# Seven-product block pairs in the w_out product of a two-layer decoder trunk

## The chip, the cores and the metric

The kernel runs on one core of a Trainium2 chip. The metric is the device time of one execution in microseconds; the median of three runs of the kernel before is 1481.37 us.

## The reference

One sequence of 512 tokens, model width 1024, passes two layers, and a last RMSNorm. All inputs are float32. Cut to what matters here:

```
h = rmsnorm(x, g_mix);  z = h @ w_in      # q, k, v | ret q, k, v, g | gate_a | gate_b
A = sliding-window attention(q, k, v)     # width 512
r = retention(ret q, k, v), normed per head, * silu(g)   # width 1024
mixed = sigmoid(gate_a) * (A @ w_a) + sigmoid(gate_b) * (r @ w_b)
x = x + mixed @ w_out                     # 1024 x 1024: the product that is changed
x = x + relu(rmsnorm(x, g_mlp) @ w_up)**2 @ w_down       # 1024 -> 4096 -> 1024
```

## The kernel before

**Layout.** Activations lie transposed: 128 rows of the width on the partitions, 512 tokens along a row. A width of 1024 is eight chunks of 128 rows (`KD = 8`), and a product makes one output chunk of 128 x 512 in one PSUM bank by eight steps over the chunks of its input.

**Three products for one.** Every operand is split into a high and a low part of fewer bits (`split`, and `split_until` for the weights: ScalarE writes the high part, VectorE the rest). `products` multiplies high by high, high by low and low by high, so a step is three matmuls with 512 columns, and an output chunk is 24 of them. The large products take most of the time.

**Weights.** `unit_order` lists all weight units (128 x 1024 numbers, 512 KB) in the order of their use. `unit` hands out the next one and has the following ones loaded (`load_until`, on SyncE's queue) and split (`split_until`) up to three ahead. Raw units, high parts and low parts have three buffers each, so the split of a unit waits until TensorE has done with the one three places earlier. `chunk` makes one output chunk from a unit, `group` four chunks together from four units, `two_chunks` two chunks from two units.

**Block pairs in the up product.** A pair of output chunks over the input's two halves and the tokens' two halves is a 2 x 2 block product. `narrow_pair` forms it from seven half-size products instead of eight, in the Winograd form of Strassen's scheme: sums and differences of weight blocks (`add_part`, VectorE), of input blocks (`sum_input`, kept in slots as `by_form`), and seven products of four steps with 256 columns, added up in three banks a, b and e. After a's first product ScalarE copies a into b, so that b goes on from it. The kernel uses this for one pair of w_up in each layer; `wide_pair` is a variant with a different split of operands, for the other pairs. The four weight parts of a pair come from two raw units.

**The stage around the change, in each layer.** `values` and the retention end; then four chunks of gate_b (`gate`, kept in `gates`), the first half of w_b as a group, four more gate chunks, and the second half of w_b as four chunks. `put_mixed` makes m, the mixed output, from each w_b chunk (in a temporary of its own) and splits it into slots (`ms`). x has served as storage for the gated attention (`mixed`) and is read back from memory for the residual. Then w_out: a group of four chunks and four single chunks. `put_x` adds a chunk to x, scales and splits it as the next input (`scaled_input`: ScalarE and VectorE), and adds up its squares (`squared_input`). Sums of x for the up product follow, then a group of four w_up chunks during which the inverse RMS is formed (`Rms.finish`, a reciprocal on VectorE), then the pairs of w_up among chunks of w_down.

**Order.** The order of instructions on each engine is set when the program is built: a scheduler of the framework places what the program issues, by its own estimates. On the chip each engine goes through its list in that order. Large buffers (`big`, 128 x 2 x 512) come from a pool of six, slots from nine tiles of four (`Slots`).

Of the kernel before, what the change touches and what calls it, by code (L numbers as in the profile page):

```python
# [12 lines left out]
F32R = mybir.dt.float32r  # L13
# [39 lines left out]
BETWEEN = (0, 2, 4, 5)  # L53


def unit_order():

    order = [("w_in", i) for i in range(4 + 2 + 8 + 2 + 4 + 2)]
    order += [("w_in", i) for i in range(22, 26)]
    order += [("w_a", i) for i in range(4)]  # L60
    order += [("w_in", i) for i in range(26, 42)]
    order += [("w_b", i) for i in range(4)]
    order += [("w_in", i) for i in range(42, 46)]
    order += [("w_b", i) for i in range(4, 8)]
    order += [("w_out", i) for i in range(8)]
    for what, q, i in mlp_sequence():
        if what == "first":
            order += [("w_up", u) for u in range(4)]
        elif what == "pair":
            order += [("pair", 8 * q + 2 * i, part) for part in range(4)]  # L70
        elif what == "down":
            order += [("w_down", 8 * q + 2 * i + u) for u in range(2)]
        else:
            order += [("w_down", 8 * q + u) for u in range(8)]
    return order
# [48 lines left out]
def decoder(ctx, tc, xT, x_first, w_in, w_a, w_b, w_out, w_up, w_down, tables, decay, band, triangles, g_last, out):  # L124
# [17 lines left out]
    def big(name, dtype=F32):  # L142
        return tmp.tile([P, 2, T], dtype, tag="big", name=name, bufs=6)
# [16 lines left out]
    slots = Slots([const.tile([P, 4, T], F32R, name=f"r{i}") for i in range(9)])  # L160
# [43 lines left out]
    def load_part(i):  # L204
        layer, _, j, part = order[i]
        if part == 0:
            raws[i] = raw_tile()
            nc.sync.dma_start(raws[i][:, LEFT], w_up[layer, j][:, LEFT])
            raws[i + 3] = raw_tile()
            nc.sync.dma_start(raws[i + 3], w_up[layer, j + 1])  # L210
        elif part == 1:
            raws[i] = big("raw2").rearrange("p a t -> p (a t)")
            nc.sync.dma_start(raws[i][:, RIGHT], w_up[layer, j][:, RIGHT])
# [15 lines left out]
    def split_until(n):  # L229
        while state["split"] < min(n, len(order)):  # L230
# [6 lines left out]
            if homes and i >= len(order) - len(homes):  # L237
                home = homes[len(order) - 1 - i]
                hi, lo = (home[:, 2 * a : 2 * a + 2, :].rearrange("p a t -> p (a t)") for a in range(2))
            else:  # L240


                first = (ASIDE, ASIDE) if paired else (0, 0)
                if paired and wide(order[i][2]):
# [266 lines left out]
    def layer_body(layer):  # L511
# [3 lines left out]
        def rstd():  # L515
            return rms_mix.value

# [474 lines left out]
        gates = []  # L992

        def gate_tile(c):
            if c % 2 == 0:
                two = big("gb")
                gates.extend(two[:, j, :] for j in range(2))
# [30 lines left out]

        source = xT if layer == 0 else spill
        for c in range(KD):  # L1030
            nc.sync.dma_start(x[:, c, :], source[:, c, :])

        def put_x(c):
            def put(ps):
                nc.vector.tensor_tensor(x[:, c, :], x[:, c, :], ps, ALU.add)
                scaled_input(c, g_mlp)
                squared_input(c, g_mlp)
# [14 lines left out]
        H = T // 2  # L1052
        sums = [slots.four() for _ in range(4)]
        by_form = [
            t[0].rearrange("p a (b t) -> p (a b) t", t=H).rearrange("p (j k s) t -> p j k s t", k=2, s=2) for t in sums
        ]

        def parts_of_forms(ks, j):
            t = by_form[2 * (j // 2) + ks // 2]
            return [t[:, :, :, s, :] for s in range(2)]  # L1060

        def sum_input(ks):

            b = [big("xg") for _ in range(2)]
            for i in range(2):
                for part, g in ((0, ks + i), (1, ks + i + 4)):
                    col = g_mlp * KD + g
                    nc.scalar.activation(b[part][:, i, :], x[:, g, :], AF.Copy, scale=gain[:, col : col + 1])
            (b11, b12), (b21, b22) = ((t[:, :, :H], t[:, :, H:]) for t in b)
            f = [big("sums").rearrange("p a (b t) -> p (a b) t", t=H) for _ in range(2)]  # L1070
            t1, t2, t3, t4 = f[0][:, 0:2, :], f[0][:, 2:4, :], f[1][:, 0:2, :], f[1][:, 2:4, :]
            nc.vector.tensor_tensor(t1, b12, b11, ALU.subtract)
            nc.vector.tensor_tensor(t2, b22, t1, ALU.subtract)
            split(*parts_of_forms(ks, 0), f[0].rearrange("p (j k) t -> p j k t", k=2))
            nc.vector.tensor_tensor(t3, b22, b12, ALU.subtract)
            nc.vector.tensor_tensor(t4, b21, t2, ALU.subtract)
            split(*parts_of_forms(ks, 2), f[1].rearrange("p (j k) t -> p j k t", k=2))

        def form(j):
            return [by_form[2 * (j // 2) + k // 2][:, j % 2, k % 2, :, :] for k in range(4)]  # L1080

        def block(half, tokens):
            at = slice(tokens * H, tokens * H + H)
            return [xhl[:, :, k, at] for k in range(4 * half, 4 * half + 4)]
# [19 lines left out]

        def narrow_pair(pool, step):
            def multiply(ps, weights, left, moving, start=True):
                hi, lo = weights
                cols = [slice((0 if left else 4 * P) + k * P, (0 if left else 4 * P) + (k + 1) * P) for k in range(4)]
                pairs = [((hi[:, c], lo[:, c]), (m[:, 0, :], m[:, 1, :])) for c, m in zip(cols, moving)]
                products(ps, pairs, start, True, not start)  # L1110

            b, a, e = (bank(pool, "mm")[:, :H] for _ in range(3))
            eu, z = temp("eu"), big("z")
            part = unit("pair", layer)
            multiply(a, part, True, block(0, 0))
            ins = nc.scalar.activation(b, a, AF.Copy).ins  # L1120
            step(ins)
            multiply(e, part, False, form(0))
            ins = nc.scalar.activation(eu[:, :H], e, AF.Copy).ins
            step(ins)
            part = unit("pair", layer)
            multiply(b, part, True, form(1), False)
            ins = nc.scalar.activation(eu[:, H:], b, AF.Copy).ins
            step(ins)
            multiply(a, part, False, block(1, 0), False)
            ins = nc.vector.scalar_tensor_tensor(z[:, 0, :H], a, 0.0, rms_mlp.value[:, :H], ALU.max, ALU.mult).ins  # L1130
            step(ins)
            part = unit("pair", layer)
            multiply(b, part, True, form(2), False)
            ins = nc.vector.tensor_tensor(z[:, 1, H:], b, eu[:, :H], ALU.add).ins  # L1134
            step(ins)
            multiply(e, part, False, block(1, 1), False)
            ins = nc.vector.tensor_tensor(z[:, 0, H:], e, eu[:, H:], ALU.add).ins
            step(ins)
            part = unit("pair", layer)
            multiply(b, part, True, form(3), False)  # L1140
            later = rms_mlp.value[:, H:].unsqueeze(1).broadcast_to([P, 2, H])
            nc.vector.scalar_tensor_tensor(z[:, :, H:], z[:, :, H:], 0.0, later, ALU.max, ALU.mult)
            nc.vector.scalar_tensor_tensor(z[:, 1, :H], b, 0.0, rms_mlp.value[:, :H], ALU.max, ALU.mult)
            return z
# [66 lines left out]
        def pair(q, i, late):  # L1211
# [11 lines left out]
            z = wide_pair(c == FIRST_WIDE + 2, i == 0 and q > 1, pool, step) if wide(c) else narrow_pair(pool, step)  # L1223
# [19 lines left out]
        def first_hooks():  # L1243
            def at1():
                rms_mlp.finish()
                sum_input(2)

            return {0: lambda: (rms_mlp.prepare(), sum_input(0)), 1: at1}

        for what, q, i in mlp_sequence():  # L1250
            if what == "first":
                late = group("w_up", layer, xs, [put_up] * 4, first_hooks())
            elif what == "pair":
                pair(q, i, late)
                if (q, i) == (3, 3):
                    for t in sums:
# [52 lines left out]
def _w_in_units(w):  # L1309
# [24 lines left out]
    units += _units_chunks(w, O_GB + r(D))  # L1334
    return units

# [55 lines left out]
def _laid_out(x, g_mix, w_in, sinks, w_a, w_b, w_out, g_mlp, w_up, w_down, g_final):  # L1392
# [13 lines left out]
        "w_b": _stack(w_b, _half_grouped),  # L1406
        "w_out": _stack(w_out, _half_grouped),
# [26 lines left out]
```

## Time and profile before

| what | value |
|---|---|
| runs | 1482.1, 1481.3, 1481.37 us; median 1481.37 us |
| profiled execution, first to last instruction | 1480.1 us |
| instructions of the profiled execution | 18928 |
| TensorE busy | 1473.5 us, 100% |
| TensorE loading weights | 1240.8 us, 84% |
| VectorE busy | 1097.6 us, 74% |
| ScalarE busy | 765.1 us, 52% |
| mean granted TensorE clock | 0.999 |
| HBM | 102 GB/s over the span |

The profiled execution is one of its own; its span is the time between its first and its last instruction, and the runs count 1.3 us more in the median. Busy times of matmuls overlap, as they are pipelined: the spacing of their starts tells what they cost, not their duration. Lines are those of the kernel before, L299 to L301 being the three matmuls of `products`. PE is TensorE, PEld its weight loads, DVE VectorE, ACT ScalarE, SP SyncE.

### The profile page before, as it was taken

The page shows a single profiled execution, that of the slowest core. Times are in us where ns is not written, and L with a number is a line of the kernel's source. Part 1 is how long each engine was busy: PE and PEld are TensorE (multiplying, and loading weights), DVE is VectorE, ACT ScalarE, POOL GpSimd, SP SyncE. Part 2 cuts the span into 40 slices and gives each one's busy share as a digit, 9 for nine tenths or more (in the row PEclk, how much of TensorE's full clock was granted, in tenths as well). Part 3 has the DMA queues.
Part 4 walks back from the last instruction along what each step waited for, and adds up shares of the span by engine and source line. Part 5 has one row for each costly group of instructions (what it writes and reads, how often), then busy time and mean ns, then how long its engine had stood idle before and what let it go on. Part 6 is the DMA issues. An engine that isn't in the chain of part 4 may idle for free.

```text
span 1480.1 us, 18928 instructions
## 1 busy us (share of the span) xinstructions
PE 1473.5 (100%) x7106; PEld 1240.8 (84%) x7106; DVE 1097.6 (74%) x1786; ACT 765.1 (52%) x1212; POOL 3.7 (0%) x14
## 2 busy tenths in 40 slices
PE   9999999999999999999999999999999999999998
PEld 7888888888888888888888888888888888888887
DVE  7998668764688787777678975786648877787763
ACT  6656355642555445444455743556327554444553
POOL 0000000000000000000000000000000000000000
PEclk9999999999999999999999999999999999999999
DMA  6422322234323332334443233232443233333341
GB/s 225 132 90 86 93 82 89 74 126 128 100 72 114 100 114 88 107 91 130 162 128 94 86 99 87 87 100 76 128 119 102 80 99 91 108 115 110 91 141 58
DMA packets 51980, 155.57 MB, mean 105 GB/s; under 512 B 6320, under 2 KB 6448, under 8 KB 51888
## 3 DMA queue, kind: packets, MB, share of 16 engines
q1 hardware_dynamic: 51600, 153.83, 34.2%
q8 instruction: 56, 0.92, 0.3%
q10 hardware_dynamic: 288, 0.52, 0.1%
q14 instruction: 36, 0.29, 0.1%
HBM read 147.51 MB, written 4.19 MB: 102 GB/s over the span
## 4 chain that ended last, share of the span: by engine, by line
PE 100%; POOLq 0%; DVE 0%; ACT 0%; issue 0%; ACTq 0%
PE mm L299 24%; PE mm L300 24%; PE mm L301 24%; PE mm L1155 11%; PE mm L1156 6%; PE rv L299 2%; PE rv L301 2%; PE rv L300 2%; PE score L696 1%; PE r L299 1%; PE r L301 1%; PE r L300 1%; PE pT L651 0%; PE pv L677 0%; PE pv L678 0%; PE warm L278 0%
## 5 line engine op out<-in xcount | busy, mean ns | idle before, releaser
L253 ACT ACTIVATE hi<-raw 128x1024 fp32r<-128x1024 f32 (+1 forms) x314 | 316.9, 1014 | 435.2 <-PE mm L300 241.0
L254 DVE TENSOR_TENSOR lo<-raw,hi 128x1024 fp32r<-128x1024 f32 (+1 forms) x315 | 365.4, 1164 | 155.6 <-ACT hi L253 154.9
L300 PE MATMUL mm<-r,hi 128*128 128x512 f32 (+1 forms) x704 | 270.8, 385 | 0.0
L299 PE MATMUL mm<-xhl,hi 128*128 128x512 f32 (+1 forms) x696 | 268.6, 388 | 0.0
L300 PE MATMUL mm<-xhl,hi 128*128 128x512 f32 (+1 forms) x696 | 268.4, 388 | 0.0
L299 PE MATMUL mm<-r,hi 128*128 128x512 f32 (+1 forms) x704 | 268.2, 385 | 0.0
L301 PE MATMUL mm<-xhl,lo 128*128 128x512 f32 (+1 forms) x696 | 267.1, 388 | 0.0
L301 PE MATMUL mm<-r,lo 128*128 128x512 f32 (+1 forms) x704 | 266.3, 384 | 0.0
L301 PEld LDWEIGHTS mm<-r,lo 128*128 128x128 f32 x704 | 132.2, 188 | 26.7
L300 PEld LDWEIGHTS mm<-r,hi 128*128 128x128 f32 x704 | 132.2, 188 | 25.6
L299 PEld LDWEIGHTS mm<-r,hi 128*128 128x128 f32 x704 | 131.7, 188 | 26.0 <-DVE z L1134 0.2
L299 PEld LDWEIGHTS mm<-xhl,hi 128*128 128x128 f32 x696 | 131.1, 188 | 26.0 <-ACT xhl L309 0.7
L301 PEld LDWEIGHTS mm<-xhl,lo 128*128 128x128 f32 x696 | 130.8, 188 | 24.8
L300 PEld LDWEIGHTS mm<-xhl,hi 128*128 128x128 f32 x696 | 130.8, 188 | 24.6
L1155 PE MATMUL mm<-r,hi 128*128 128x512 f32 x416 | 146.7, 391 | 0.0
L1156 PE MATMUL mm<-r,lo 128*128 128x256 f32 x416 | 115.3, 277 | 0.0
L1155 PE MATMUL mm<-xhl,hi 128*128 128x512 f32 x312 | 110.4, 391 | 0.0
L1155 PEld LDWEIGHTS mm<-r,hi 128*128 128x128 f32 x416 | 78.1, 188 | 16.2
L1156 PE MATMUL mm<-xhl,lo 128*128 128x256 f32 x312 | 86.6, 277 | 0.0
L1156 PEld LDWEIGHTS mm<-r,lo 128*128 128x128 f32 x416 | 78.1, 188 | 1.8
L1155 PEld LDWEIGHTS mm<-xhl,hi 128*128 128x128 f32 x312 | 58.6, 188 | 11.9
L1156 PEld LDWEIGHTS mm<-xhl,lo 128*128 128x128 f32 x312 | 58.6, 188 | 1.7
(256 smaller groups left out, 2077.1 us busy)
## 6 DMA issues: line engine op xcount, KB each, us to landing
raw<-w_in_in SPq DMA_DIRECT2D x89, 512.0 KB, 3.6
raw<-w_down_in SPq DMA_DIRECT2D x64, 512.0 KB, 3.6
raw<-w_up_in SPq DMA_DIRECT2D x36, 512.0 KB, 3.6
raw<-w_up_in SPq DMA_DIRECT2D x56, 256.0 KB, 2.8
raw<-w_b_in SPq DMA_DIRECT2D x16, 512.0 KB, 3.6
raw<-w_out_in SPq DMA_DIRECT2D x16, 512.0 KB, 3.8
raw<-w_a_in SPq DMA_DIRECT2D x8, 512.0 KB, 3.6
x<-xT_in SPq DMA_DIRECT2D x15, 256.0 KB, 3.7
```

The source lines that it names most:

```text
L253: nc.scalar.activation(hi[:, at], raw[:, at], AF.Copy)
L254: last_low[:] = [nc.vector.tensor_tensor(lo[:, at], raw[:, at], f32(hi[:, at]), ALU.subtract).ins]
L299: nc.tensor.matmul(ps, ah, bh, start=start and i == 0, stop=False, **more)
L300: nc.tensor.matmul(ps, ah, bl, start=False, stop=False, **more)
L301: nc.tensor.matmul(ps, al, bh, start=False, stop=stop and i == n - 1, **more)
L696: nc.tensor.matmul(ps[:, g * w : (g + 1) * w], q_s[g][:, c, at], part[:, keys], start=i == 0, stop=i == 1)
L1155: nc.tensor.matmul(both, hi[:, c], m, start=start and k == 0, stop=False, **more)
L1156: nc.tensor.matmul(ps[:, :H], lo[:, c], m[:, 0, :], start=False, stop=k == 3 and start, **more)
```

## The change

The w_out product of each layer is made as two plain chunks (`two_chunks`), a block pair with seven products (`narrow_pair`), two plain chunks and another pair. `narrow_pair`, `sum_input` and their helpers move ahead of the stage and take their input blocks, their sums and their last step as arguments, so that w_out and w_up share them. The pair's weights come from w_out's raw units by the same additions as before. The sums of m are formed in two halves, after each half of w_b; for this the output chunks of w_b and of gate_b come in the order 0, 1, 4, 5, 2, 3, 6, 7 (`CROSSED`), and the plain chunks of w_out go through m in that order. m is written over its gate's tile. The scaled input and the squares of a pair's two chunks follow after the pair. There are ten slot tiles instead of nine and seven large buffers instead of six; a scratch area of dynamic DMAs is made smaller (4096).

```diff
+H = T // 2
+CROSSED = (0, 1, 4, 5, 2, 3, 6, 7)
...
-    order += [("w_out", i) for i in range(8)]
+    order += plain("w_out", 2) + pairs("w_out", 2) + plain("w_out", 4, 6) + pairs("w_out", 6)
...
-        return tmp.tile([P, 2, T], dtype, tag="big", name=name, bufs=6)
+        return tmp.tile([P, 2, T], dtype, tag="big", name=name, bufs=7)
...
-    slots = Slots([const.tile([P, 4, T], F32R, name=f"r{i}") for i in range(9)])
+    slots = Slots([const.tile([P, 4, T], F32R, name=f"r{i}") for i in range(10)])
...
+        def narrow_pair(pool, step, form, block, put):
...
+            b, a, e = (bank(pool, "mm")[:, :H] for _ in range(3))
+            eu, z = temp("eu"), big("z")
+            part = unit("pair", layer)
+            multiply(a, part, True, block(0, 0))
+            ins = nc.scalar.activation(b, a, AF.Copy).ins
+            step(ins)
+            multiply(e, part, False, form(0))
+            ins = nc.scalar.activation(eu[:, :H], e, AF.Copy).ins
+            step(ins)
+            part = unit("pair", layer)
+            multiply(b, part, True, form(1), False)
+            ins = nc.scalar.activation(eu[:, H:], b, AF.Copy).ins
+            step(ins)
+            multiply(a, part, False, block(1, 0), False)
+            step(put(0, FIRST, a, z).ins)
+            part = unit("pair", layer)
+            multiply(b, part, True, form(2), False)
+            ins = nc.vector.tensor_tensor(z[:, 1, SECOND], b, eu[:, :H], ALU.add).ins
+            step(ins)
+            multiply(e, part, False, block(1, 1), False)
+            ins = nc.vector.tensor_tensor(z[:, 0, SECOND], e, eu[:, H:], ALU.add).ins
+            step(ins)
+            part = unit("pair", layer)
+            multiply(b, part, True, form(3), False)
+            put(slice(0, 2), SECOND, z[:, :, SECOND], z)
+            put(1, FIRST, b, z)
+            return z
...
         def put_mixed(c):
             def put(ps):
-                m = temp("m")
-                nc.vector.tensor_tensor(m, ps, gates[c], ALU.mult)
-                nc.vector.tensor_tensor(m, m, mixed[c], ALU.add)
+                m = gates[c]
+                nc.vector.tensor_tensor(m, ps, m, ALU.mult)
+                nc.vector.tensor_tensor(m, m, mixed[CROSSED[c]], ALU.add)
                 hi, lo = slots.one(), slots.one()
                 split(view(hi), view(lo), m)
-                ms[c] = (hi, lo)
+                ms[CROSSED[c]] = (hi, lo)
...
         all_of(group("w_b", layer, rT, [put_mixed(c) for c in range(4)]))
+        homes_m = [forms_home(), None, forms_home(), None]
+        by_form_m = [h and h[1] for h in homes_m]
+        sum_input(by_form_m, gate_tiles[:2], 0)
         for c in range(4, KD):
             gate_tile(c)
             chunk("w_in", layer, xs, gate(gates[c]))
...
+        homes_m[1::2] = [forms_home() for _ in range(2)]
+        by_form_m[:] = [h[1] for h in homes_m]
+        sum_input(by_form_m, gate_tiles[2:], 2)
...
+        def add_to_x(c):
+            def put(i, at, src, z):
+                own = x[:, c + i, at] if isinstance(i, int) else x[:, c : c + 2, at]
+                return nc.vector.tensor_tensor(own, own, src, ALU.add)
...
-        all_of(group("w_out", layer, mT, [put_x(c) for c in range(4)]))
-        for c in range(4, KD):
-            chunk("w_out", layer, mT, put_x(c))
+        for c in range(0, KD, 4):
+            two_chunks("w_out", layer, [mT[k] for k in CROSSED], [put_x(c), put_x(c + 1)])
+            narrow_pair(ps_aux, lambda ins: None, form_of(by_form_m), block_m, add_to_x(c + 2))
+            for i in (2, 3):
+                next_input(c + i)
```

More of the change, by code (lines that the diff above doesn't have):

```diff
@@ L243, in split_until @@
                 first = (ASIDE, ASIDE) if paired else (0, 0)
-                if paired and wide(order[i][2]):
+                if paired and order[i][4] == "w_up" and wide(order[i][2]):
                     first = (ASIDE, 0)
@@ new lines, in scaled_pair, with form_of, block @@
+        def scaled_pair(ks, which):
+            b = [big("xg") for _ in range(2)]
+            for part, g in ((0, ks), (1, ks + 4)):
+                for i in range(2):
+                    col = which * KD + g + i
+                    nc.scalar.activation(b[part][:, i, :], x[:, g + i, :], AF.Copy, scale=gain[:, col : col + 1])
+            return b
+        def form_of(by_form):
+            return lambda j: [by_form[2 * (j // 2) + k // 2][:, j % 2, k % 2, :, :] for k in range(4)]
+        def block(half, tokens):
+            at = slice(tokens * H, tokens * H + H)
+            return [xhl[:, :, k, at] for k in range(4 * half, 4 * half + 4)]
@@ new lines, in layer_body, with multiply @@
+        FIRST, SECOND = slice(0, H), slice(H, T)
+        def narrow_pair(pool, step, form, block, put):
+            def multiply(ps, weights, left, moving, start=True):
+                hi, lo = weights
+                cols = [slice((0 if left else 4 * P) + k * P, (0 if left else 4 * P) + (k + 1) * P) for k in range(4)]
+                pairs = [((hi[:, c], lo[:, c]), m if isinstance(m, tuple) else (m[:, 0, :], m[:, 1, :])) for c, m in zip(cols, moving)]
+                products(ps, pairs, start, True, not start)
+            b, a, e = (bank(pool, "mm")[:, :H] for _ in range(3))
[25 more added lines that the diff above has]
+            return z
@@ L1045, in layer_body @@
         for k in range(KD):
             slots.give(*ms.pop(k))
[L1052 to L1084, printed above, removed]
+        for t, _ in homes_m:
+            slots.give(*t[1])
+        def positive(i, at, src, z):
+            factor = rms_mlp.value[:, at]
+            if not isinstance(i, int):
+                factor = factor.unsqueeze(1).broadcast_to([P, 2, H])
+            return nc.vector.scalar_tensor_tensor(z[:, i, at], src, 0.0, factor, ALU.max, ALU.mult)
@@ L1103, in up_home @@
             return big("uhi", F32R), big("ulo", F32R), []
[L1105 to L1144, printed above, removed]
         def wide_pair(first, close, pool, step):
```

88 lines of the change are left out of this document (62 added, 26 removed).

## The prediction, as it stood before the run

> **What bounds the kernel now.** I read the page first: the span, TensorE's share, the granted clock and the chain that ended last.
>
> ```profile
> span 1480.1 us, 18928 instructions
> ...
> PE 1473.5 (100%) x7106; PEld 1240.8 (84%) x7106; DVE 1097.6 (74%) x1786; ACT 765.1 (52%) x1212; POOL 3.7 (0%) x14
> ...
> PEclk9999999999999999999999999999999999999999
> ...
> PE 100%; POOLq 0%; DVE 0%; ACT 0%; issue 0%; ACTq 0%
> ```
>
> The chain is TensorE from end to end, at nine tenths of its clock or more in every slice. So the time is the number of matmuls times their spacing, plus whatever makes TensorE wait, and today hardly anything does. An edit pays only by fewer or shorter matmuls, and loses by any new wait of TensorE. Next, the busy time by stage of layer 0: second half of the w_b product with its gates, the w_out product, the first w_up group, the first block pair of w_up.
>
> ```profile
> core 0: us, PE busy (x) PEld busy (x) DVE busy (x) ACT busy (x) POOL busy (x), PEclk, DMA share, GB/s
> ...
> 319.00:362.70 43.70, 43.70 (x195) 36.18 (x194) 25.27 (x33) 16.15 (x21) 0.00 (x0) 1.00 0.46 133
> 362.70:406.20 43.50, 43.50 (x194) 36.02 (x192) 28.96 (x37) 23.38 (x32) 0.00 (x0) 1.00 0.35 107
> 406.20:428.40 22.20, 22.20 (x99) 18.39 (x98) 18.94 (x22) 10.69 (x12) 0.00 (x0) 1.00 0.24 76
> 428.40:447.00 18.60, 18.60 (x135) 17.39 (x134) 16.17 (x25) 15.27 (x27) 0.00 (x0) 1.00 0.27 82
> ```
>
> TensorE has no room in any of them. VectorE has 14.5 us free in the w_out stage (43.50 less 28.96) and only 3.3 us in the group after it (22.20 less 18.94): there its cover is thin. ScalarE has 20 us free in w_out, but what will matter is the order in which it works, not its share.
>
> The prices of matmuls come from starts, since a duration of 0.39 us overlaps the next one. The timeline of TensorE, at the ends of two stretches without a gap:
>
> ```profile
> start us, us, engine line op out<-in xcount [idle before <-releaser]
> ...
> 362.68 0.39 PE L299 MATMUL mm<-r,hi 128*128 128x512 f32 x1
> ...
> 406.20 0.39 PE L299 MATMUL mm<-xhl,hi 128*128 128x512 f32 x1
> ...
> 428.41 0.28 PE L299 MATMUL mm<-xhl,hi 128*128 128x256 f32 x1
> ...
> 436.89 0.40 PE L1155 MATMUL mm<-xhl,hi 128*128 128x512 f32 x1
> ```
>
> From 362.68 to 406.20 stand the 192 matmuls of w_out with 512 columns: 43.52 / 192 = 0.2267 us each. From 428.41 to 436.89 stand 72 of the 84 half-width matmuls of the one narrow pair that each layer has already: 8.48 / 72 = 0.1178 us each, without a gap.
>
> **The matmuls (the gain).** Of the eight w_out chunks of a layer four stay whole, in two groups of two; the other four become two block pairs of seven products. A pair is 7 x 4 x 3 = 84 half-width matmuls in place of 2 x 8 x 3 = 48 wide ones. Per layer 96 x 0.2267 = 21.76 us go and 168 x 0.1178 = 19.79 us come: 1.97 us saved, 3.94 us in both layers, if nothing waits.
>
> The Trainium skill speaks against this price ("TensorE: Matmul & The Clock Gate", "Back-to-back issue gap"): sustained streams cost about 81 ns at 128 columns and 131 ns at 512, so half the columns are far from half the price. Drawn straight between its two figures, an estimate, 256 columns cost 98 ns, and a layer would pay 168 x 98 ns = 16.4 us for 96 x 131 ns = 12.6 us, a loss of 3.9 us. The rows above disagree with it (0.1178 against 0.2267, ratio 0.52), and I take the rows.
>
> **A new wait of TensorE in each pair.** A pair needs a's first product copied into b by ScalarE before b's second part may be added. In the built program ScalarE's order after each two plain chunks is: the high half of the pair's third weight part (1024 columns), then for each of the two chunks its scaled input and its square (512 columns each), and only then that copy. The high half itself waits for a buffer that the last plain matmuls release, so nothing in this row can start before the plain chunks end; call that T. Rows of the same kinds on ScalarE, and the copy in the narrow pair of today:
>
> ```profile
> 386.83 1.04 ACT L253 ACTIVATE hi<-raw 128x1024 fp32r<-128x1024 f32 x1
> 387.78 0.71 ACT L309 ACTIVATE xhl<-x 128x512 fp32r<-128x512 f32 x1
> 388.39 0.62 ACT L383 ACTIVATE sq<-x 128x512 f32<-128x512 f32 x1
> 388.91 0.72 ACT L309 ACTIVATE xhl<-x 128x512 fp32r<-128x512 f32 x1
> 389.53 0.62 ACT L383 ACTIVATE sq<-x 128x512 f32<-128x512 f32 x1
> 390.05 1.05 ACT L253 ACTIVATE hi<-raw 128x1024 fp32r<-128x1024 f32 x1
> ...
> 428.43 1.06 ACT L253 ACTIVATE hi<-raw 128x1024 fp32r<-128x1024 f32 x1 [4.38 <-PE mm L300]
> 430.02 0.37 ACT L1120 ACTIVATE mm<-mm 128x256 f32<-128x256 f32 x1 [0.53 <-PE mm L301]
> ```
>
> By starts the half costs 0.95, then 0.61, 0.52, 0.62 and 0.52: 3.22 us. The half at 428.43 began 0.02 after the last matmul that read its buffer's group (the next one starts at 428.41). Today's copy, which stood behind that half alone, began at 430.02, 0.20 after the twelfth narrow matmul (428.41 + 12 x 0.1178 = 429.82), and b was not wanted until twelve more had passed, so nobody waited. In the new order the copy starts at T + 0.02 + 3.22 = T + 3.24 and ends at T + 3.61. How soon TensorE goes on after a releaser shows where it waited for a weight piece:
>
> ```profile
> 435.81 1.22 DVE L254 TENSOR_TENSOR lo<-raw,hi 128x1024 fp32r<-128x1024 f32 x1
> ...
> 437.08 0.19 PEld L1156 LDWEIGHTS mm<-xhl,lo 128*128 128x128 f32 x1
> ...
> 437.12 0.34 PE L1156 MATMUL mm<-xhl,lo 128*128 128x256 f32 x1
> 437.31 0.40 PE L1155 MATMUL mm<-xhl,hi 128*128 128x512 f32 x1
> ```
>
> The piece ended at 437.03, its load started at 437.08, and the matmul behind it can have begun only 0.1178 before its successor, at 437.19: 0.16 us after the releaser. So b's second part starts at T + 3.77. TensorE has 24 half-width matmuls to do in between (2.83 us); in the first pair of a layer one of them has been put ahead of T, which leaves 2.71. The waits are 1.06 and 0.94 us, 2.00 us a layer, 4.00 us in all: as much as the gain. Bounds: 0 for a copy that finds ScalarE free, 4.8 us if each step takes a tenth of a microsecond more. I take 4.00, since every term is a row of its own kind and the order is fixed. (The two x additions that the scaled inputs need end before T + 1.1 by the row of 0.69 us, so they do not decide.)
>
> **VectorE and the first pairs of w_up.** What VectorE now does per layer in addition: eight weight additions of 512, three more low weight halves of 1024, and for m's sums eight subtractions and four low halves. The first half of m's sums lies beside the four gate chunks, where the first stage row leaves 18 us free. The rest falls between the last w_b chunk and the w_up group. Its prices, by starts:
>
> ```profile
> 417.30 0.39 PE L405 MATMUL ssq<-sl,ones 128*128 128x512 f32 x1
> ...
> 419.47 0.69 ACT L406 ACTIVATE rstd<-ssq,x 128x512 f32<-128x512 f32 x1
> ...
> 420.20 3.35 DVE L407 RECIPROCAL rstd<-rstd 128x512 f32<-128x512 f32 x1 [0.78 <-ACT rstd L406]
> 423.46 0.63 DVE L219 TENSOR_TENSOR raw<-raw 128x512 f32<-128x512 f32 x1
> ...
> 429.53 1.23 DVE L254 TENSOR_TENSOR lo<-raw,hi 128x1024 fp32r<-128x1024 f32 x1 [3.61 <-ACT hi L253]
> ...
> 434.26 0.42 DVE L1130 SCALAR_TENSOR_TENSOR z<-mm,rstd 128x256 f32<-128x256 f32 x1 [0.28 <-PE mm L301]
> 434.61 0.68 DVE L226 TENSOR_TENSOR raw<-raw 128x512 f32<-128x512 f32 x1
> 435.20 0.69 DVE L227 TENSOR_TENSOR raw<-raw 128x512 f32<-128x512 f32 x1
> ...
> 436.94 0.42 DVE L1137 TENSOR_TENSOR z<-mm,eu 128x256 f32<-128x256 f32 x1
> ```
>
> ```profile
> 382.60 2.05 DVE L1035 TENSOR_TENSOR x<-x,mm 128x512 f32<-128x512 f32 x3 [1.31 <-PE mm L301]
> 384.56 0.75 DVE L310 SCALAR_TENSOR_TENSOR xhl<-x,xhl 128x512 fp32r<-128x512 f32 x1
> 385.22 0.69 DVE L1035 TENSOR_TENSOR x<-x,mm 128x512 f32<-128x512 f32 x1
> ```
>
> 0.60 for 512 columns (434.61 to 435.20 to 435.81), 1.13 for 1024 (435.81 to 436.94), 0.35 for 256, 0.66 for a scaled one (384.56 to 385.22), 3.26 for the reciprocal. From the end of the second two plain chunks to the start P of the first w_up pair TensorE takes 3.77 + 5.65 + 1.41 (rest of the pair) + 21.76 (96 wide) + 0.45 (two for the sum of squares) = 33.0 us. VectorE's list for that stretch in the built program is 21 of 512, 11 of 1024, 4 of 256 and 4 scaled: 12.6 + 12.4 + 1.4 + 2.6 = 29.0 us, with some 3 us of waits at its start for the pair's results. It ends about 1 us ahead of P. In w_out itself the same sum leaves each weight piece 2 us or more ahead of TensorE, so I cost that at nothing; without this cover each late piece costs what it is late.
>
> Then comes the reciprocal. Today the sum of squares is multiplied at 417.30, 11 us ahead of the pair at 428.41, and the reciprocal is over 5 us ahead. In the built program that matmul stands five wide ones (1.13 us) before the pair: with 0.20 to ScalarE and its 0.69 us the reciprocal starts at P - 0.24 and ends its slot at P + 3.02. Behind it in VectorE's order stand, before the low half of the next pair's first weights ends: two additions, two weight halves of 1024 and 512, two scaled evictions, a 256-wide one, an addition, and that half (1.22 by its row): 1.20 + 1.13 + 0.60 + 1.32 + 0.35 + 0.60 + 1.22 = 6.42, so P + 9.44, with 0.16 P + 9.60. TensorE wants it at P + 8.48 + 0.23 = P + 8.71: 0.9 us late. Today the same piece is 0.07 us late (437.31 - 437.12 less 0.1178), with VectorE's idle 3.61 us at 429.53 as the reserve that goes. Counted on in the same way, the second weight part comes about 0.4 us and the next group's 0.1 us late: 1.4 us a layer, 2.8 us in all. Bounds: 0 (VectorE keeps up) and 2.2 us a layer; I take 1.4.
>
> Ten slots instead of nine, seven large buffers instead of six, the crossed order of w_b's and the gates' chunks, and the m written over the gate tile move no instruction onto the path: the first two plain chunks read m in the crossed order, so the last m is needed 9.5 us after its chunk ends, and its chain (two evictions, halves, sums) is about 5 us long by the prices above. DMA stands at a share of 0.35 in w_out; the same weight bytes come, in smaller pieces, and a free buffer stays the condition for each.
>
> **The sum.** Span 1480.1 - 3.94 + 4.00 + 2.8 = 1483.0 us. The median of the runs, 1481.37, lies 1.3 us over the profiled span, so the time is 1484.2 us (+0.19%). About 0.2%, or 3 us, is what a measurement of this kernel can tell from no change: 1478.4 to 1484.3.
>
> **The rivals.**
> Main case (0.45): both waits appear; 1481.4 to 1486.6 by their bounds. Half of it lies over 1484.3.
> The copy alone (0.17): the pairs wait 4.0 us, VectorE keeps up; 1481.37 - 3.94 + 4.00 = 1481.4. For it: VectorE's margin is a matter of one microsecond in 29. Against: the reciprocal is tied to a matmul five places ahead of the pair.
> Nothing waits (0.16, faster): if ScalarE's row ahead of the copy ends 1 us sooner, by halves that start before T or by steps at 0.5 us, the gain stays: 1477.4, up to 1478.4 with small waits. For it: today's narrow pair has no gap in 72 matmuls. Against: the four extra steps stand in the row.
> VectorE falls behind (0.20, slower): if its list ends more than 0.8 us later than worked out, P passes before it is through and the reciprocal and all behind it slip; 2 us of slip cost 2 us a layer, 1484.2 + 4.0 = 1488.2. For it: 29 of 33 us are busy and waits between engines are counted in one place only.
> Half-width matmuls are bound by their weight loads (0.02, slower):
>
> ```profile
> L301 PEld LDWEIGHTS mm<-r,lo 128*128 128x128 f32 x704 | 132.2, 188 | 26.7
> ```
>
> At 0.188 us each, 168 of them cost 31.6 us against 21.76: 9.8 us a layer, 1501. Against it stand the 72 in a row at 0.1178.
>
> **The numbers.** Faster: 0.16 and 0.02 from the edge of the second case, 0.18. Slower: 0.20 + 0.02 and 0.25 of the main case, 0.47. The rest, 0.35, is no change. The range from 1478.0 to 1488.5 leaves out part of the faster case and the tail of the slower ones; the main case alone would be 1481.4 to 1486.6.
>
> **What would show it.** The profile after must show 168 more half-width matmuls a layer at 0.118 us, 96 fewer wide ones, and in each w_out pair one hole of about 1 us before b's second part, with the copy released late because ScalarE was at scaled inputs and squares. At the second w_up pair of each layer TensorE should wait for low weight halves, with VectorE busy without a break since the reciprocal. I am wrong if those holes are absent (then the time is near 1477), or if holes stand elsewhere, above all at weight pieces inside w_out.

## The result, and the profile after

Over 20 runs of each kernel the changed one takes 1483.8 us in the median and the kernel before 1481.45 us: a ratio of 1.0015, with a 95% interval of 1.0009 to 1.0022. That is 2.35 us more, which lies inside the 0.2% that the prediction counts as no change, and 0.4 us below the 1484.2 us forecast. The interval leaves out 1, so the loss is small but clear.

The rows of the page after that answer to those of before, and then its view of what TensorE waited for (engine and line, whom it waited for, microseconds in total, times, the longest):

```profile
span 1481.5 us, 19321 instructions
...
PE 1470.9 (99%) x7250; PEld 1243.8 (84%) x7250; DVE 1135.7 (77%) x1846; ACT 782.0 (53%) x1240; POOL 3.8 (0%) x14
...
PEclk9999999999999999999999999999999999999999
...
PE 93%; issue 5%; DVE 1%; ACT 0%; DMA 0%; POOLq 0%; DVEq 0%; SPq 0%
```

```profile
engine line waited for: us in total, times, longest us
PE mm L303 <- ACT mm L574: 3.0, 4, 0.8
PE mm L1196 <- DVE lo L258: 1.3, 4, 0.5
PE warm L282 <- DVE ones L277: 1.0, 1, 1.0
```

TensorE is busy 2.6 us less (1473.5 before), in 144 more matmuls that the profile recorded, and yet the span is longer. The chain of before was TensorE at 100%; now VectorE has 1% of it, and 5% are "issue". That share is no hole of TensorE. Nearly all of it is one stretch of 71.4 us near the end (1406.0 to 1477.4), in which the chain follows POOL's queue back from the last instruction while TensorE goes on working. It is as large in the repaired version below, so the chain is no measure of the holes here. The waits name both causes. Before, the view had only the row for the start of the kernel. Now there are four waits for ScalarE's copy (L574), two in each layer, and four for a low weight half of VectorE (L258). The view counts a wait only from the modelled end of the matmul before it, so a hole is longer than its row here: holes are read from starts below.

The first hole, in the first pair of layer 0: TensorE's rows, then ScalarE's.

```profile
start us, us, engine line op out<-in xcount [idle before <-releaser]
...
372.67 0.28 PE L304 MATMUL mm<-r,hi 128*128 128x256 f32 x1
...
375.26 0.28 PE L305 MATMUL mm<-r,lo 128*128 128x256 f32 x1
376.34 0.38 PE L303 MATMUL mm<-r,hi 128*128 128x256 f32 x1 [0.81 <-ACT mm L574]
376.56 0.28 PE L304 MATMUL mm<-r,hi 128*128 128x256 f32 x1
```

```profile
372.69 1.06 ACT L257 ACTIVATE hi<-raw 128x1024 fp32r<-128x1024 f32 x1 [3.59 <-PE mm L304]
373.66 0.71 ACT L313 ACTIVATE xhl<-x 128x512 fp32r<-128x512 f32 x1
374.27 0.62 ACT L384 ACTIVATE acc<-x 128x512 f32<-128x512 f32 x1
374.79 0.71 ACT L313 ACTIVATE xhl<-x 128x512 fp32r<-128x512 f32 x1
375.41 0.61 ACT L387 ACTIVATE sq<-x 128x512 f32<-128x512 f32 x1
375.93 0.36 ACT L574 ACTIVATE mm<-mm 128x256 f32<-128x256 f32 x1
```

The last plain matmul that the high half waits for has its successor at 372.67; that is T. The half (L257) starts at T + 0.02, then come scaled input, square, scaled input, square, and only then, at T + 3.26, the copy. Of TensorE's 23 half-width matmuls behind T the last starts at 375.26, and the one behind it must begin 0.118 ahead of the row 376.56, at 376.44, which is T + 3.77. From 375.26 to 376.56 are 1.30 us, where two spacings, 0.24, were due: a hole of 1.07 by the unrounded starts. The other pair of the layer shows 0.96, and layer 1 the same two.

The second place, at the second w_up pair of layer 0, VectorE's rows and then TensorE's:

```profile
427.37 3.36 DVE L411 RECIPROCAL rstd<-rstd 128x512 f32<-128x512 f32 x1 [0.59 <-ACT rstd L410]
...
435.64 1.22 DVE L258 TENSOR_TENSOR lo<-raw,hi 128x1024 fp32r<-128x1024 f32 x1
```

```profile
427.58 0.28 PE L303 MATMUL mm<-xhl,hi 128*128 128x256 f32 x1
...
436.06 0.40 PE L1195 MATMUL mm<-xhl,hi 128*128 128x512 f32 x1
436.92 0.39 PE L1196 MATMUL mm<-xhl,lo 128*128 128x256 f32 x1 [0.46 <-DVE lo L258]
437.15 0.40 PE L1195 MATMUL mm<-xhl,hi 128*128 128x512 f32 x1
```

The reciprocal starts at 427.37, 0.21 us ahead of the first w_up pair (427.58), after VectorE stood idle for 0.59. The low half that the second pair wants ends at 435.64 + 1.22 = 436.86. From 436.06 to 437.15 TensorE takes 1.09 us for one wide and one half-width matmul, 0.345 by the prices: it goes on 0.745 us late. Two smaller holes follow (0.465 at 441.7, and 0.29 us at the next group), 1.5 us a layer. VectorE's view shows it without idle time from the start of the reciprocal until 451.6.

### The profile page after: what moved, and what is told of

Read it like the earlier page. It is cut to its first block, busy times and chain, and to the rows that moved or that the text cites. A ratio compares the mean times of both kernels' runs of the same rounds, so it can differ in the third digit from the quotient of the medians.

```text
span 1481.5 us, 19321 instructions
## 1 busy us (share of the span) xinstructions
PE 1470.9 (99%) x7250; PEld 1243.8 (84%) x7250; DVE 1135.7 (77%) x1846; ACT 782.0 (53%) x1240; POOL 3.8 (0%) x14
## 4 chain that ended last, share of the span: by engine, by line
PE 93%; issue 5%; DVE 1%; ACT 0%; DMA 0%; POOLq 0%; DVEq 0%; SPq 0%
PE mm L303 22%; PE mm L304 22%; PE mm L305 22%; PE mm L1195 10%; PE mm L1196 5%; PE rv L303 2%; PE rv L304 2%; PE rv L305 2%; PE score L776 1%; PE r L303 1%; PE r L304 1%; PE r L305 1%; PE pT L731 0%; DVE lo L258 0%; PE pv L757 0%
## 5 line engine op out<-in xcount | busy, mean ns | idle before, releaser
L257 ACT ACTIVATE hi<-raw 128x1024 fp32r<-128x1024 f32 (+1 forms) x322 | 324.2, 1008 | 419.0 <-PE mm L304 215.1
L258 DVE TENSOR_TENSOR lo<-raw,hi 128x512 fp32r<-128x512 f32 (+1 forms) x323 | 373.5, 1159 | 130.2 <-ACT hi L257 129.2
L304 PE MATMUL mm<-r,hi 128*128 128x512 f32 (+1 forms) x800 | 295.6, 370 | 0.0
L303 PE MATMUL mm<-r,hi 128*128 128x512 f32 (+1 forms) x800 | 292.1, 371 | 3.0 <-ACT mm L574 3.0
L305 PE MATMUL mm<-r,lo 128*128 128x512 f32 (+1 forms) x800 | 290.5, 370 | 0.0
L303 PEld LDWEIGHTS mm<-r,hi 128*128 128x128 f32 x800 | 149.7, 188 | 29.3 <-ACT mm L574 3.8
L305 PEld LDWEIGHTS mm<-r,lo 128*128 128x128 f32 x800 | 150.0, 188 | 26.9 <-DVE lo L258 0.9
L304 PEld LDWEIGHTS mm<-r,hi 128*128 128x128 f32 x800 | 150.1, 188 | 25.2
L1195 PEld LDWEIGHTS mm<-r,hi 128*128 128x128 f32 x416 | 78.1, 188 | 16.3
L1196 PEld LDWEIGHTS mm<-r,lo 128*128 128x128 f32 x416 | 78.1, 188 | 2.5 <-DVE lo L258 1.2
```

The source lines that it names most:

```text
L257: nc.scalar.activation(hi[:, at], raw[:, at], AF.Copy)
L258: last_low[:] = [nc.vector.tensor_tensor(lo[:, at], raw[:, at], f32(hi[:, at]), ALU.subtract).ins]
L303: nc.tensor.matmul(ps, ah, bh, start=start and i == 0, stop=False, **more)
L304: nc.tensor.matmul(ps, ah, bl, start=False, stop=False, **more)
L305: nc.tensor.matmul(ps, al, bh, start=False, stop=stop and i == n - 1, **more)
L1195: nc.tensor.matmul(both, hi[:, c], m, start=start and k == 0, stop=False, **more)
```

## The experiments

All times are medians, each with the kernel before run on the same chip (1481.3 to 1481.6 us); "after" is the changed kernel, 1483.8 us. My theory was that of the prediction: a gain of 3.94 us, eaten by two costs that have nothing to do with each other, ScalarE's order in the pairs and VectorE's lateness at w_up. The rivals: the matmuls are not as cheap as thought, the waits belong to the pair itself, or what is repaired in one place comes back in another.

**The copy first.** The plain chunks are added to x as before, but their scaled inputs and squares are queued behind the pair's copies.

```diff
 def put_x(c):
     ...
-        next_input(c)
 ...
-narrow_pair(ps_aux, lambda ins: None, form_of(by_form_m), block_m, add_to_x(c + 2))
+turn = iter([c, None, c + 1])
+def after(ins):
+    k = next(turn, None)
+    if k is not None:
+        with tc.issue_after(ins):
+            next_input(k)
+narrow_pair(ps_aux, after, form_of(by_form_m), block_m, add_to_x(c + 2))
```

> ScalarE's copy of a into b is put ahead of the scaled inputs and squares of the two plain chunks; nothing else is edited. Theory (the wait in each w_out pair is that copy standing behind four steps of ScalarE): all four waits go, 1.07 and 0.96 us a layer, 4.06 us in all, 1483.8 - 4.06 = 1479.7. Rival one (what is late moves on): the second pair ends 0.96 us sooner, VectorE's list up to the first w_up pair has that much less time, and the waits at the second w_up pair grow by up to 0.96 us a layer: 1483.8 - 4.06 + 1.9 = 1481.6. Rival two (the wait belongs to the pair's own chain and not to ScalarE's order): holes and time stay, 1483.8.

Measured: 1479.5 us, 0.9986 of before (0.9977 to 0.9995), 4.3 us less than after. ScalarE's rows, and what TensorE still waited for:

```profile
373.02 1.06 ACT L257 ACTIVATE hi<-raw 128x1024 fp32r<-128x1024 f32 x1 [3.59 <-PE mm L304]
374.48 0.37 ACT L574 ACTIVATE mm<-mm 128x256 f32<-128x256 f32 x1 [0.40 <-PE mm L305]
374.76 0.72 ACT L313 ACTIVATE xhl<-x 128x512 fp32r<-128x512 f32 x1
375.38 0.62 ACT L384 ACTIVATE acc<-x 128x512 f32<-128x512 f32 x1
```

```profile
PE mm L1203 <- DVE lo L258: 1.3, 4, 0.5
PE warm L282 <- DVE ones L277: 1.0, 1, 1.0
```

The copy starts at 374.48 instead of 375.93, and the row of four waits for it is gone. The 1.3 us for L258 stay as they were: nothing is given back. The first theory holds, and both rivals fall.

**The sum of squares early.** The matmuls of the last quarter of the first w_up group are queued behind those of the sum of squares.

```diff
+SUM_BEFORE = 6
...
 for j in range(2):
     k = 2 * u + j
+    first = name == "w_up" and k == SUM_BEFORE
     for c, ps in enumerate(banks):
         ...
-        products(...)
+        with tc.issue_after(last_sum[0]) if first else nullcontext():
+            products(...)
```

> The matmuls for the sum of squares are put ahead of the last quarter of the first w_up group, so that the reciprocal can start some 3 us sooner; the list of VectorE is the same. Theory (VectorE's whole list is what is late, and the reciprocal's place costs only the 0.59 us for which VectorE stands idle ahead of it): the first of the three waits at the second w_up pair, 0.745 us with its echo, shrinks by 0.6, the two others stay: 1.2 us in all, 1482.6. Rival one, as the prediction had it (the reciprocal's place is the cause): all three waits go, 1.5 us a layer, 1480.8. Rival two (the weight halves that the reciprocal now stands ahead of come late): no gain, 1483.8 or more, with new holes in the first w_up pair.

Measured: 1481.3 us (0.9998 of before, 0.9989 to 1.0006), 2.5 us less than after; between the two theories.

```profile
425.05 3.35 DVE L417 RECIPROCAL rstd<-rstd 128x512 f32<-128x512 f32 x1
...
435.11 1.22 DVE L260 TENSOR_TENSOR lo<-raw,hi 128x1024 fp32r<-128x1024 f32 x1
```

The reciprocal starts at 425.05 with no idle time ahead of it, and the low half ends at 436.33. The first wait loses the expected 0.6 us; 0.11 is left. VectorE's list did not stay quite the same: a weight addition and a weight half that stood ahead of the reciprocal now stand behind it, so at this wait only the 0.59 us of idle time is won. But the second shrinks to 0.25 and the third is gone too, which I had not expected: with the reciprocal earlier, the built order also has the third and the fourth low half of the group's outputs each behind one more weight half. So 1.15 us a layer go, not 0.6 and not 1.5.

**Which of VectorE's steps count.** Two runs take 0.60 us steps from it, ahead of the reciprocal and behind it.

```diff
 # one_add_less
-square_sum(acc_of[which], x[:, k, :], k == 0)
+square_sum(acc_of[which], x[:, k, :], k == 0, which % 2 == 1 and k == 6)   # no addition
 # low_left_out
-split(view(hi), view(lo), t)
+nc.scalar.activation(view(hi), t, AF.Copy)
```

> One addition of VectorE a layer is left out, that of the seventh chunk's square to the sum of squares (so that chunk is missing from the sum). It stands ahead of the reciprocal; no other instruction changes its place on any engine. Theory (ahead of the reciprocal VectorE has slack, since the reciprocal waits for the matmul of the sum of squares, whose place in TensorE's order is fixed): its idle time ahead of the reciprocal grows from 0.59 to 1.19 us, the three waits stay at 1.5 us a layer, 1483.8. Rival (VectorE's whole list is what is late): the first wait shrinks by 0.60 us a layer, 1482.6.

> The low halves of the first w_up group's four outputs are left out, on every engine (whatever stood in their place before is multiplied). VectorE has four steps of 0.60 us a layer less behind the first wait at the second w_up pair, and ScalarE nothing more, other than in the run in which it wrote zeros. Theory (behind the reciprocal VectorE's load is what is late): the first wait (0.745 us) stays, the second and third (0.465 and 0.29 us) go, 1.5 us in all, 1482.3. Rival (the second and third wait have another cause): 1483.8.

Measured: 1483.5 us for the first (1.0015 of before, 1.0006 to 1.0024), its three waits unchanged, as the theory has it. But its number for the idle time was wrong: VectorE's idle time ahead of the reciprocal is 0.63 us, and not 1.19, since 0.44 us of the step's time went into a wait for ScalarE earlier, at 411.6. So the run took little load away just ahead of the reciprocal and is weak evidence by itself. Stronger is the row of after: VectorE stood idle for 0.59 us there, until the step of ScalarE behind the matmul was done.

The second run took 1482.0 us (1.0005 of before, 0.9996 to 1.0015), 1.8 less than after, and has only the first wait left. The low half that the second wait is for, in after and then in this run:

```profile
440.44 1.22 DVE L258 TENSOR_TENSOR lo<-raw,hi 128x1024 fp32r<-128x1024 f32 x1
```

```profile
439.33 1.22 DVE L258 TENSOR_TENSOR lo<-raw,hi 128x1024 fp32r<-128x1024 f32 x1
```

It starts 1.1 us sooner, as two of the four steps stood ahead of it. So behind the reciprocal VectorE's load is what is late: 2.4 us of steps less in a layer took 0.75 us of waits away. (Behind the second wait some matmuls change places too in the built order, so the third wait is a less clean test.) Ahead of the reciprocal, up to the idle time there, the load costs nothing, since the reciprocal waits for a matmul of a fixed place.

**The same steps on POOL and on ScalarE.** The low halves of low_left_out are the subtraction that the output needs; the question was who else could do it.

```diff
-split(view(hi), view(lo), t)
+nc.scalar.activation(view(hi), t, AF.Copy)
+nc.gpsimd.tensor_tensor(view(lo), t, f32(view(hi)), ALU.subtract)   # low_on_pool
+nc.scalar.activation(view(lo), t, AF.Copy, scale=0.0)               # low_on_scalar
```

> The low halves of the first w_up group's four outputs are computed by POOL instead of VectorE; they lie behind the first of the three waits at the second w_up pair. Theory (VectorE's load decides): VectorE loses four steps of 0.60 us a layer, the first wait (0.745 us) stays, the second and third (0.465 and 0.29) go: 1.5 us in all, 1482.3. Rival (POOL's work slows VectorE's beside it by as much as it saves): VectorE's rows in that stretch are longer than 0.69 and 1.22 us, the waits stay, 1483.8 or more.

> The low halves of the first w_up group's four outputs are not subtracted by VectorE; ScalarE writes zeros there (so this correction is left out). That takes four steps of 0.60 us a layer from VectorE behind the first wait, as the run on POOL did, without POOL. Theory (behind the reciprocal VectorE's load is what is late): the first wait (0.745 us) stays, the second and third (0.465 and 0.29) go, 1.5 us in all, 1482.3; and then what POOL's run lost is POOL's slowing of VectorE, 2.0 us. Rival (these waits do not hang on VectorE's load): 1483.8.

Measured: 1484.3 us on POOL (1.0019 of before, 1.0010 to 1.0028), 0.5 us worse than after and 2.4 worse than without these steps. POOL's row, and VectorE's beside it:

```profile
437.15 7.55 POOL L1176 TENSOR_TENSOR r<-up,r 128x512 fp32r<-128x512 f32 x4 [434.51 <-PE mm L304]
...
440.45 1.39 DVE L258 TENSOR_TENSOR lo<-raw,hi 128x1024 fp32r<-128x1024 f32 x1
441.77 1.78 DVE L1161 SCALAR_TENSOR_TENSOR z<-z,rstd 128x512 f32<-128x512 f32 x1
443.47 0.41 DVE L1161 SCALAR_TENSOR_TENSOR z<-mm,rstd 128x256 f32<-128x256 f32 x1
443.80 2.58 DVE L258 TENSOR_TENSOR lo<-raw,hi 128x1024 fp32r<-128x1024 f32 x2
```

The same kinds of steps in after:

```profile
431.18 1.81 DVE L258 TENSOR_TENSOR lo<-raw,hi 128x1024 fp32r<-128x1024 f32 x2
...
441.58 0.69 DVE L1161 SCALAR_TENSOR_TENSOR z<-z,rstd 128x512 f32<-128x512 f32 x1
```

A scaling step of 512 columns with two operands in SBUF (z and rstd) takes 1.78 us instead of 0.69, and a pair of low halves 2.58 instead of 1.81. The evictions that read an accumulator (mm) keep their 0.41 us. The Trainium skill ("SBUF — State Buffer", "Who interferes with whom") says the same: a VectorE instruction with two inputs in SBUF contends with a POOL instruction that reads SBUF, and one with a single such input does not. So POOL cost 2.4 us against leaving the steps out, more than the 1.8 us that they are worth on VectorE. On ScalarE the run took 1483.5 us (1.0015 of before, 1.0006 to 1.0023) and settles little: the second and third wait are gone, but TensorE has a new one of 0.5 us, for a copy of ScalarE (eu, L1226), which now stands behind the four more steps.

```profile
444.71 0.50 PE L1196 MATMUL mm<-xhl,hi 128*128 128x512 f32 x1 [0.34 <-ACT eu L1226]
```

**Parts of the change.** In three runs pairs are turned back into plain chunks; all else stays.

```diff
-order += plain("w_out", 2) + pairs("w_out", 2) + plain("w_out", 4, 6) + pairs("w_out", 6)
+order += plain("w_out", 8)                                            # sums_only
+order += plain("w_out", 2) + pairs("w_out", 2) + plain("w_out", 4, 8) # first_pair_only
+order += plain("w_out", 6) + pairs("w_out", 6)                        # second_pair_only
```

> Everything of the change but the pairs: the four pairs' chunks are plain two-chunk groups again, while m's sums (eight subtractions and the halves a layer), the crossed order, the tenth group of slots and the seventh large buffer stay; the sums are computed and not used. Theory (the side work costs nothing on the path): 1481.5, without waits at the second w_up pair, because the last rows of x come in time. Rival (the sums' load on VectorE and ScalarE is what makes the reciprocal late): waits of up to 1.5 us a layer there, 1484.5.

> Of the two pairs of a layer only the first is kept; the second is two plain chunks again. Half of the matmuls' gain (1.97 us over both layers), the first pair's wait (1.07 us a layer, 2.14). Theory (the waits at the second w_up pair come from the second pair, whose columns of x come last and through more steps): none there, 1481.5 - 1.97 + 2.14 = 1481.7. Rival (they come from VectorE's added load in general): half of them, 0.75 us a layer, 1483.2.

> Of the two pairs of a layer only the second is kept. Half of the gain (1.97), the second pair's wait (0.96 us a layer, 1.92). Theory (the second pair alone makes the reciprocal late): the full 1.5 us a layer at the second w_up pair, 1481.5 - 1.97 + 1.92 + 3.0 = 1484.4. Rival (VectorE's added load in general): half of that, 1482.9.

Measured, with the ratio to before: 1481.1 us (0.9997, 0.9988 to 1.0006), 1481.2 (0.9999, 0.9990 to 1.0008) and 1483.5 (1.0014, 1.0005 to 1.0022). The reciprocal of layer 0 in the three, in that order:

```profile
420.66 3.35 DVE L411 RECIPROCAL rstd<-rstd 128x512 f32<-128x512 f32 x1 [0.46 <-ACT rstd L410]
```

```profile
420.59 3.35 DVE L411 RECIPROCAL rstd<-rstd 128x512 f32<-128x512 f32 x1 [0.38 <-ACT rstd L410]
```

```profile
428.26 3.36 DVE L411 RECIPROCAL rstd<-rstd 128x512 f32<-128x512 f32 x1 [0.58 <-ACT rstd L410]
```

Sums, crossed order and buffers cost nothing. With the first pair alone the reciprocal starts some 7 us earlier and there is no wait at w_up; with the second alone it is as late as in after and all three waits are there (0.74, 0.49, 0.28 us). So it is the second pair that makes the reciprocal late, and not VectorE's added load as such, which is as large with the first pair alone (1126.2 us busy against 1125.1). In TensorE's list the last matmul of the sum of squares stands 36 matmuls ahead of the first w_up pair in the first two runs and five ahead in the third. That the built order puts it there because the second pair's columns of x come last is likely, but not shown. Against the sums of the expectations the second and third run are 0.5 and 0.9 us faster; 0.4 us of each is in the first run already.

**The price of half-width matmuls.** In the kernel before, 22 of the 24 matmuls of every w_out chunk are cut in two.

```diff
+for s in (slice(0, T),) if first or last else (slice(0, H), slice(H, T)):
+    nc.tensor.matmul(ps[:, s], a, b[:, s], start=first, stop=last)
```

> The kernel before, with 22 of the 24 matmuls of each w_out chunk cut into two of 256 columns: 704 half-width ones in place of 352 wide ones, the same arithmetic. By the rows of starts: 704 x 0.1178 - 352 x 0.2267 = +3.1 us, 1484.6. By the interpolated figures of the Trainium skill (TensorE: Matmul & The Clock Gate, Back-to-back issue gap; 98 and 131 ns): 704 x 0.098 - 352 x 0.131 = +22.9 us, 1504.3. If weight loads set the pace (0.188 us each): 704 x 0.188 - 79.8 = +52.6 us, 1534.

Measured: 1486.1 us (1.0031 of before, 1.0019 to 1.0043), 4.6 us more.

```profile
PE 1477.2 (100%) x7458; PEld 1258.4 (85%) x7458; DVE 1097.8 (74%) x1786; ACT 765.3 (52%) x1212; POOL 3.7 (0%) x14
...
361.69 0.62 PE L300 MATMUL mm<-r,hi 128*128 128x512 f32 x3
362.14 0.40 PE L300 MATMUL mm<-r,lo 128*128 128x256 f32 x2
...
407.32 0.40 PE L300 MATMUL mm<-r,lo 128*128 128x512 f32 x1
407.55 0.40 PE L308 MATMUL mm<-xhl,hi 128*128 128x512 f32 x1
```

From 361.69 to 407.55 lie 352 half-width and 16 wide matmuls: (45.86 - 16 x 0.2267) / 352 = 0.1200 us each, 2% above the 0.1178 of the pairs, and TensorE never waits. Neither the pace of the weight loads (1534 us) nor the estimate from the Trainium skill's figures (1504.3) comes near. Why these cost 2% more I did not try.

**Both repairs.**

> Both edits at once: the copy ahead of scaled inputs and squares (alone 1479.5) and the sum of squares ahead of the last quarter of the first w_up group (alone 1481.3, 2.5 us less than the changed kernel). Theory (two independent costs, each gone with its cause): they add up, 1479.5 - 2.5 = 1477.0, with 0.36 us a layer of waits left at the second w_up pair; that is the whole gain of the matmuls, 1481.5 - 3.94 = 1477.5, and a little. Rival (VectorE is so full that the microsecond won in each second pair is asked back when the reciprocal is early too): waits at the second w_up pair grow by up to 0.96 us a layer, 1478.9.

Measured: 1476.7 us, 0.9968 of before (0.9956 to 0.9981): 7.1 us less than after and 4.9 less than before. This version beats both kernels.

```profile
span 1474.9 us, 19317 instructions
...
PE 1468.2 (100%) x7250; PEld 1243.2 (84%) x7250; DVE 1135.0 (77%) x1846; ACT 781.6 (53%) x1240; POOL 3.8 (0%) x14
...
PE warm L284 <- DVE ones L279: 1.0, 1, 1.0
PE mm L305 <- ACT xhl L315: 0.4, 1, 0.4
```

Of the waits in this view there is left the start of the kernel and one of 0.4 us in its first microseconds; by starts, 0.36 us a layer remain at the second w_up pair, as expected. TensorE is busy for 100% of the span again. The repairs add up; the rival's wait does not come.

## Why the prediction was right, step by step

The time fell into the main case, and for its reasons.

**The bound and the price.** TensorE stayed the bound. The pairs' matmuls cost 0.1177 us (372.67 to 375.26 in 22 steps), as taken from today's pair. The estimate from the Trainium skill's figures for sustained streams ("TensorE: Matmul & The Clock Gate", "Back-to-back issue gap"), by which half the columns would have lost 3.9 us a layer, does not hold for this kernel: these rows disagree with it, and so does the run in halves, which it put at 1504.3 us and which took 1486.1.

**The copy.** Start of the copy T + 3.26 (worked out: T + 3.24), b's second part T + 3.77 (T + 3.77), holes of 1.07 and 0.96 us (1.06 and 0.94), 4.06 us in all (4.00). Taking the cause away gave back 4.3 us. The upper bound of 4.8 us does not follow from its own words: the half and four steps, each a tenth of a microsecond longer, would be 0.5 us more in each of four pairs, 6.0 us in all.

**VectorE and w_up.** The reciprocal started at P - 0.21 (P - 0.24); the first late half ended at P + 9.28 (P + 9.44). The three waits are 0.745, 0.465 and 0.29 us (0.9, 0.4 and 0.1), 1.5 us a layer (1.4). What the prediction left open, the runs showed: the reciprocal's place comes from the second pair alone, and the load that counts is the one behind it.

**What costs nothing.** Slots, buffers, crossed order and the sums: 1481.1 us in the run with these alone. There is no hole at a weight piece inside w_out.

**The sum.** It was right to 0.4 us in the end, and that closeness is partly luck, as its two parts were not: two errors of opposite sign nearly cancel. The span came out 1.4 us longer than before's, not 2.9, and the median lies 2.3 us over the span, not 1.3. The first sum of squares shows why (views of the tile "ssq", of before and of after; the times are of the first and the last):

```profile
L405 PE MATMUL ssq<-sh,ones x12: 389/389/389, 27.0 to 1149.2; 128*128 128x512 f32 x12
```

```profile
L409 PE MATMUL ssq<-sh,ones x12: 389/389/389, 25.9 to 1156.6; 128*128 128x512 f32 x12
```

Before's profiled execution reached it 1.1 us later than after's, in the first 27 us, which the change does not touch. So its span was a poor base, by about the error of both terms. What the prediction took for a fixed 1.3 us was the median of the runs set against one execution: in each of the twenty runs of after the time lies 1.7 to 1.8 us over that run's own span, and the profiled execution was the fastest of them (1483.25 us). A small term was also missing: before had 0.17 us a layer of gaps of its own at the second w_up pair, which vanish in the larger waits. From the last sum of squares of the mixer to the first of the next layer (in the second layer to the last matmul), where all of the pairs lie, TensorE's starts are 1.33 and 1.35 us further apart than before; the steps give (-3.94 - 0.34 + 4.06 + 3.0) / 2 = 1.39 a layer.

The chances were less well placed than the time: 0.47 stood on more than 1484.3 us and 0.35 on what the prediction calls no change, and the time came out 0.5 us under that edge.

One remainder stays open in part. For the version with both repairs the same steps give -3.94 - 0.34 + 0.72 (waits left) = -3.6 us; TensorE's starts in those stretches show -4.1, and the median -4.9. Of the missing 0.5 us some 0.3 are in the run with the sums alone: without any pair, its starts in the same stretches are 0.2 and 0.1 us closer together than before's. Why, and what the rest of the median is, no run shows.

## What to carry to other kernels

A gain of fewer matmuls is only had if the small helper steps that the new form needs stand early in their engine's queue: here one copy behind four unhurried steps in each pair cost as much as the matmuls saved. Write out the engine's order around the new form, count it against the time that the matmuls give it, and tie the unhurried steps behind the urgent one. When an engine is late, ask where in its list: here it stood idle ahead of a step with a fixed release, where less load would have won nothing, and behind that step less load took waits away.

## What the runs showed of the hardware

Beside VectorE's work, POOL's subtraction of 512 columns took about 1.9 us (7.55 for four, by its rough row) where VectorE takes 0.60, and a step of VectorE with two operands in SBUF was stretched from 0.69 to 1.78 us, so that here work moved to an idle engine gained nothing. And the half-width matmuls that a chunk was cut into cost 0.1200 us each, those of the pairs 0.1178.
